# One decoder layer on one core: keys as the standing operand of a small network's first layer, and the last transposes of x1 moved into the last product

## The chip, the cores and the metric

The kernel runs on one core of a Trainium2 chip. The metric is the device time of one execution in microseconds (us); less is better. Each time named is a median of runs, and a trace of one profiled execution is shown beside it. The engines are called PE (TensorE; PEld is its weight load), DVE (VectorE), ACT (ScalarE), POOL (GpSimd) and SP (the queue that starts most DMAs). They run side by side, each works its own list of instructions strictly in order, and they wait for one another by semaphores.

## The reference

One transformer layer over 256 rows of 1024 numbers. What matters here is the compressed branch of mixer A: overlapping blocks of 32 keys (and values) go through a small two-layer network, whose output takes part in an attention. The rest is large products in float32 accuracy.

```python
def compress_blocks(k, pe, w1, w2):
    b, seq, g, d = k.shape
    n_cmp = (seq - CMP_BLOCK) // CMP_STRIDE + 1          # 15 blocks of 32 rows
    idx = jnp.arange(n_cmp)[:, None] * CMP_STRIDE + jnp.arange(CMP_BLOCK)[None, :]
    kb = k[:, idx] + pe[None, None, :, None, :]
    kb = jnp.transpose(kb, (0, 3, 1, 2, 4)).reshape(b, g, n_cmp, CMP_BLOCK * d)
    return jax.nn.gelu(kb @ w1) @ w2                     # (30 rows x 2048) @ (2048 x 64) @ (64 x 64)
...
        kc = compress_blocks(k_c, cmp_pe_k[layer], cmp_k_w1[layer], cmp_k_w2[layer])
        vc = compress_blocks(v_c, cmp_pe_v[layer], cmp_v_w1[layer], cmp_v_w2[layer])
...
        mixed = g_nsa * (y_nsa @ w_up_nsa[layer]) + g_moba * (y_moba @ w_up_moba[layer])
        x = x + mixed @ w_out[layer]
        h2 = rmsnorm(x, norm2_g[layer])
        u = jax.nn.relu(h2 @ w_ff1[layer])
        x = x + (u * u) @ w_ff2[layer]
    return rmsnorm(x, norm_f_g)
```

## The kernel before

**Chunks and slots.** All weights come in 60 chunks of up to 1 MB (`CHUNKS`), one after another: kva, kvb, q, qm, km, vm, gm, upn, upm, wout, ff1, ff2. A chunk is loaded into `raw` (three buffers), then split into a high part `whi` by ACT (line 107) and a low part `wlo` by DVE (line 109), so that three fast products give float32 accuracy (`mm3`, line 214). One *slot* is the run of matmuls that uses one chunk (24 or 48 of them), and it also carries the splitting of the chunk two further on. "Slot 5" is the slot of chunk 5.

**The order is written by hand.** `at(pos, f)` puts work at a share `pos` of the slot, and `run_slot` emits it between the slot's matmuls, in order of `pos`. Each engine's list is therefore what these shares make it: what stands ahead in an engine's list is done first, even while it waits.

**The small network.** `cmp_gather` (slot 3) transposes the keys and values of kva and adds the position term; the result is `kE`, 30 blocks by 16 pairs of rows, for keys (s=0) and values (s=1). `cmp_mlp1` (share 0.7 of slot 4) multiplies by `w1`: 32 float32 products with 64 columns of `w1` standing in the array and 30 columns of `kE` moving, keys in the first 64 columns of the array and values in the other 64, one sum each. Behind it come an ACT copy to `gl`, three DVE operations, a tanh on ACT and one DVE operation that writes `glr`: the gelu. `cmp_mlp2` (0.45 of slot 5) takes `glr` through the second layer: one product for the keys (`tk`, read by DVE into `bdk`) and one for the values (`tv`, read into `bdv`). A float32 product is recorded as two matmuls, a transpose as one.

**Around it in slots 4 and 5.** `split(5, ..)` and `split(6, ..)` on DVE; `transp_k(kva)` (0.1 of slot 5) transposes the keys `ks` on PE, and `split_evac` reads them out on ACT (`ksh`, `ks`) and DVE (`ksl`); `rope` on DVE; `transp_k(kvb)` (0.75 of slot 5) does the same for `kw`.

**Banks.** Small results share two PSUM banks, `tp` and `yb`, which `tp_tile` gives out in turn; large ones take the banks in `turn["acc"]`, in turn as well. A bank's next user waits until its last one has been read. `tv` is two calls behind the `ks` transposes and so falls on their bank. For the gm slots (from chunk 12) the bank `tp` joins `acc0` and `acc1`, behind them.

**x1.** `x1_rows` transposes the new residual back to rows, four 128x128 transposes for each quarter: quarter 0 in the middle of the second wout slot, quarters 1 to 3 in the middle of the second ff2 slot.

Of the kernel before, what the change touches and what calls it, by code (L numbers as in the profile page):

```python
# [33 lines left out]


K_MASK, K_COS, K_SIN, K_CMP, K_BDK, K_BDV, K_IND, K_N = 0, 128, 160, 192, 222, 254, 382, 386
S_PE, S_W2, S_N = 0, 32, 160


@with_exitstack  # L40
def hybrid_layer(ctx: ExitStack, tc: tile.TileContext, gxd, w, w1c, small, const, gf, out):
# [82 lines left out]
    sm = cp.tile([128, S_N], F32, name="sm")  # L124
    kc_ = cp.tile([128, K_N], F32, name="kc")

    glr = ap_.tile([128, 4, 32], F32, name="glr")
    pcs = ap_.tile([128, 2, 4, 32], F32, name="pcs")
    pool.memset(glr, 0.0)
    pool.memset(pcs, 0.0)  # L130
    w1 = ap_.tile([128, 2, 16, 64], F32, name="w1", tag="w1")
    xsq = ap_.tile([128, 8, 256], F32, name="xsq", tag="early")
# [12 lines left out]
    load(4)  # L145
    g1, g2 = gx[:, 0:8], gx[:, 8:16]
    pe_sb = sm[:, S_PE:S_PE + 32].rearrange("p (s l) -> p s l", s=2)
    w2 = sm[:, S_W2:S_W2 + 128]
    cmask = kc_[:, K_MASK:K_MASK + 128]
    cos = kc_[:, K_COS:K_COS + 32].rearrange("p (t d) -> p t d", t=2)  # L150
    sin = kc_[:, K_SIN:K_SIN + 32].rearrange("p (t d) -> p t d", t=2)
# [107 lines left out]
            split_events(c, (0.0, 0.45), (0.3, 0.46))  # L259


    kva = ap_.tile([128, 2, 128], F32, name="kva")
    kcd = ap_.tile([128, 2, 4, 2, 64], F32, name="kcd")
    kvb = ap_.tile([128, 2, 408], F32, name="kvb")
    vm = ap_.tile([128, 2, 512], F32, name="vm")
# [58 lines left out]
        split_evac(tp[:, None, 0:256], dst, False)  # L324


    kE = ap_.tile([128, 2, 16, 30], F32, name="kE")
    bdk = ap_.tile([128, 32], F32, name="bdk")
    bdv = ap_.tile([128, 4, 128], F32, name="bdv")
    sT = ap_.tile([128, 256], F32, name="sT")  # L330
    pcT = ap_.tile([128, 256], F32, name="pcT")
    gl = ap_.tile([128, 3, 30], F32, name="gl")
    gates = (ap_.tile([128, 56], F32, name="gates")[:, 0:48]
             .rearrange("p (b q t h) -> p b q t h", b=3, q=4, t=2))
    U = {}
# [1 line left out]
    def cmp_gather(s):  # L337
        tp = tp_tile()
        for g in range(2):
            for t in range(2):  # L340
                pe.transpose(tp[:, g * 256 + t * 128:g * 256 + t * 128 + 128],
                             kcd[:, t, 2 * s + g].rearrange("p a d -> p (a d)"), ident)
        for l2 in range(2):
            p0 = l2 * 64
            v = tp[p0:p0 + 64].rearrange("p (g i l m) -> p g l i m", g=2, l=8, m=2)
            for lh in range(2):
                ls = slice(lh * 8, (lh + 1) * 8)
                o = kE[p0:p0 + 64, s, ls, :].rearrange("p l (g i) -> p g l i", g=2)
                dve.tensor_tensor(
                    o, v[:, :, :, lh:lh + 15, l2],  # L350
                    pe_sb[p0:p0 + 64, s, None, ls, None].to_broadcast([64, 2, 8, 15]),
                    op=ALU.add)

    def cmp_mlp1():
        tp = tp_tile()
        for l in range(16):
            for s in range(2):
                mm(tp[s * 64:(s + 1) * 64, 0:30], w1[:, s, l, :], kE[:, s, l, :], l == 0, l == 15)
        act.activation(gl[:, 0], tp[:, 0:30], AF.Copy)
        dve.tensor_tensor(gl[:, 1], gl[:, 0], gl[:, 0], op=ALU.mult)  # L360
        dve.tensor_scalar(gl[:, 1], gl[:, 1], 0.044715, 1.0, op0=ALU.mult, op1=ALU.add)
        dve.tensor_tensor(gl[:, 1], gl[:, 1], gl[:, 0], op=ALU.mult)
        act.activation(gl[:, 2], gl[:, 1], AF.Tanh, scale=0.7978845608028654)
        a, b = (gl[:, i, None, :].to_broadcast([128, 4, 30]) for i in (2, 0))
        dve.scalar_tensor_tensor(glr[:, :, 0:30], a, 1.0, b, op0=ALU.add, op1=ALU.mult)

    def cmp_mlp2():
        tk = tp_tile()
        mm(tk[:, 0:32], w2[0:64, :], glr[0:64, 0, :], True, True)
        dve.tensor_tensor(bdk, tk[:, 0:32], kc_[:, K_BDK:K_BDK + 32], op=ALU.mult)  # L370
        tv = tp_tile()
        mm(tv[:, 0:128], glr[64:128].rearrange("k p c -> k (p c)"), w2[64:128, :], True, True)
        for p in range(4):
            dve.scalar_tensor_tensor(bdv[:, p, :], tv[:, 0:128], kc_[:, K_IND + p:K_IND + p + 1],
                                     kc_[:, K_BDV:K_BDV + 128], op0=ALU.mult, op1=ALU.mult)
# [8 lines left out]
    qT = ap_.tile([128, 4, 256], F32, name="qT")  # L384
    qrT, qmT, kmT = (qk_tiles(n, 4, n != "km") for n in ("qr", "qm", "km"))
    ksT, kwT = (qk_tiles(n, 1, False) for n in ("ks", "kw"))
    st4 = ap_.tile([128, 136], F32, name="st4")[:, 0:64].rearrange("p (a b) -> p a b", a=4)

    def cmp_scores():
        tp = tp_tile()  # L390
        for p in range(4):
            mm(tp[32 * p:32 * p + 32, 0:256], bdk, qT[:, p, :], True, True)
        act.activation(sT, tp[:, 0:256], AF.Copy)

    def cmp_softmax():
        tp = tp_tile()
        for t in range(2):
            pe.transpose(tp[:, t * 128:(t + 1) * 128], sT[:, t * 128:(t + 1) * 128], ident)
        s4 = tp[:, 0:256].rearrange("q (t p c) -> q t p c", t=2, p=4)[:, :, :, 0:30]
        heads = lambda a: a.rearrange("q p (h i) -> q p h i", h=2)  # L400
        for t in range(2):
            dve.tensor_tensor(heads(pcs[:, t, :, 0:30]), heads(s4[:, t]),
                              cmpm[:, t, None, None, :].to_broadcast([128, 4, 2, NCMP]), op=ALU.add)
        s = pcs.rearrange("q t p c -> q (t p) c")[:, :, 0:30].rearrange("q a (h i) -> q a h i", h=2)
        col = lambda i: st4[:, i].rearrange("q (a h) -> q a h", h=2)
        row = lambda i: col(i)[:, :, :, None].to_broadcast([128, 8, 2, NCMP])
        dve.tensor_reduce(col(0), s, op=ALU.max, axis=AX)
        dve.tensor_scalar(st4[:, 0], st4[:, 0], -1.0e30, None, op0=ALU.max)
        dve.tensor_tensor(s, s, row(0), op=ALU.subtract)
        act.activation(s, s, AF.Exp, scale=0.125)  # L410
        dve.tensor_reduce(col(1), s, op=ALU.add, axis=AX)
        dve.tensor_scalar(st4[:, 1], st4[:, 1], 1.0e-30, None, op0=ALU.max)
        dve.reciprocal(st4[:, 2], st4[:, 1])
        dve.tensor_tensor(st4[:, 3].rearrange("q (t p h) -> q t p h", t=2, p=4),
                          st4[:, 2].rearrange("q (t p h) -> q t p h", t=2, p=4),
                          gates[:, 0].rearrange("q p t h -> q t p h"), op=ALU.mult)
        dve.tensor_tensor(s, s, row(3), op=ALU.mult)
# [127 lines left out]
    for sec, c0, n in groups:  # L545
# [6 lines left out]
        for i in range(2):  # L552
            c = c0 + i
            if c == 0:
                at(0.6, load, 5)
            elif c == 1:
                at(0.88, row_squares, 0)
                at(0.88, row_sums, 0, 2, 2)
                for k in range(4):
                    at(0.89, split, 2, k, 4)  # L560
                at(1.1, row_squares, 1)
                at(1.1, row_sums, 4, 6, 2)
                at(1.1, row_sums, 0, 4, 2)
                at(1.1, row_sums, 0, 1, 1)
                for k in range(4):
                    at(1.2, split, 3, k, 4)
                at(1.3, load, 6)
                at(1.3, nc.sync.dma_start, w1, w1c)
            elif c == 2:
                at(0.75, row_norm)  # L570
            elif c == 3:
                for t in range(2):
                    at(0.0, evac_tm, "kva", t, first[t], 384)
                for k in range(2):
                    at(0.1, split, 4, k, 2, "h")
                at(0.45, cmp_gather, 0)
                for k in range(2):
                    at(0.5, split, 4, k, 2, "l")
                at(0.51, load, 7)
                at(0.6, cmp_gather, 1)  # L580
                for k in range(2):
                    at(0.7, split, 5, k, 2, "h")
            elif c == 4:
                for t in range(2):
                    at(0.0, evac_tm, "kvb", t, second[t], 408)
                at(0.1, split, 5, 0, 2, "l")
                at(0.2, rope, kva, 2)
                at(0.3, split, 5, 1, 2, "l")
                at(0.35, load, 8)
                split_events(c, (0.5, 0.55), (0.8, 0.9))  # L590
                at(0.7, cmp_mlp1)
            else:
                std_events(c)
            unit_events(c)
# [42 lines left out]
                       scale=hrstd[:, t:t + 1])  # L637

    prev = []
    turn["acc"].append("tp")  # L640
    for g in range(4):
        accs = [acc_tile(), acc_tile()]
        for i in range(2):
# [133 lines left out]
    for i in range(4):  # L777
# [11 lines left out]
            at(0.02, f, *a)  # L789
        if i == 1:  # L790
            at(0.01, open_ff)

            at(26 / 48 - 0.001, lambda: x1_rows([0], [bank("yb", "yb")]))
            at(0.9, lambda: act.dma_start(FB["gfb"], gf[None, :].to_broadcast([128, 1024])))
        if i == 3:
            outs = [acc_tile()[:, 0:256] for _ in range(2)]
# [101 lines left out]
    for i in range(15):  # L898
# [2 lines left out]
            at(0.02, f, *a)  # L901
        prev = []
        if i == 1:
            at(0.5, x1_rows, range(1, 4), [acc_tile() for _ in range(3)])
        if i == 3:
            at(0.1, rstd2)
        if i < 14:
# [23 lines left out]
def _layout(np, inp):  # L931
# [26 lines left out]
    xT = np.asarray(inp["x"])[0].T.reshape(8, 128, 256).transpose(1, 0, 2).reshape(128, 2048)  # L958
    gx = np.concatenate(cols + [xT], 1)
    cols = [np.asarray(inp[n])[0].reshape(16, 128).T for n in ("cmp_pe_k", "cmp_pe_v")]  # L960
    w2 = np.concatenate([np.asarray(inp[n])[0] for n in ("cmp_k_w2", "cmp_v_w2")], 0)
    cols += [w2, w2]
    small = np.concatenate(cols, 1)

    t = np.arange(256)
# [39 lines left out]
```

## Time and profile before

| | |
|---|---|
| median of 3 runs | 386.05 us (385.52 to 386.81) |
| the profiled execution's own time | 386.25 us |
| its span, first to last instruction | 384.4 us |
| PE busy | 375.2 us, 98% of the span |
| PEld busy | 329.1 us, 86% |
| DVE busy | 254.3 us, 66% |
| ACT busy | 205.6 us, 54% |
| POOL busy | 3.2 us, 1% |
| DMA | 66.31 MB |

The span leaves 1.85 us of the profiled time outside. Busy shares are averages over stages with different limits. A matmul's end is modelled, so matmuls that follow each other closely overlap in the rows; what a matmul costs in a stream is the distance of its start from the next start.

### The profile page before, as it was taken

Reading aid. Unit: us, or ns where it says so; the run is one execution under the profiler, and the core shown is the slowest. Engines: PE = TensorE matmul, PEld = TensorE weight load, DVE = VectorE, ACT = ScalarE, POOL = GpSimd, SP = SyncE. Lnnn points to the kernel's source line nnn. Section 1 sums busy time; section 2 is a strip of 40 time slices with the busy share of each in tenths; the row PEclk is TensorE's granted clock in tenths of the full one; section 3 lists DMA queues with packets and bytes.
Section 4 is the critical chain, followed back from the end, with each engine's and each line's share of the span. In section 5 each row is a group of like instructions: output and inputs, shape, how many; then the busy total and the mean of one; then the engine's idle time right before and its main releaser. Section 6 shows DMA issues by size and latency. Waiting matters only on the chain.

```text
span 384.4 us, 5939 instructions
## 1 busy us (share of the span) xinstructions
PE 375.2 (98%) x2404; PEld 329.1 (86%) x2404; DVE 254.3 (66%) x396; ACT 205.6 (54%) x359; POOL 3.2 (1%) x14
## 2 busy tenths in 40 slices
PE   7999999999999999999999999999999999999993
PEld 6897778878888788779999999999998888888883
DVE  3969788887966869567857656756757354344435
ACT  5974465766746747353554555565565364323412
POOL 1000000000000000000000000000000000000000
PEclk9999999999999999999999999999999999999999
DMA  7977535333533434630756644554564546545003
GB/s 243 368 304 231 208 124 205 109 111 124 206 109 112 124 140 175 217 112 7 264 224 219 220 160 175 215 188 155 206 213 143 206 186 237 198 162 188 0 2 110
DMA packets 11261, 66.31 MB, mean 173 GB/s; under 512 B 1249, under 2 KB 2785, under 8 KB 3937
## 3 DMA queue, kind: packets, MB, share of 16 engines
q1 hardware_dynamic: 10800, 65.14, 47.5%
q10 hardware_dynamic: 432, 0.79, 0.6%
q8 instruction: 19, 0.31, 0.3%
q14 instruction: 10, 0.07, 0.1%
HBM read 64.87 MB, written 1.05 MB: 172 GB/s over the span
## 4 chain that ended last, share of the span: by engine, by line
PE 90%; DVE 3%; ACT 2%; issue 2%; DMA 1%; SPq 1%; POOLq 0%; POOL 0%; DVEq 0%; ACTq 0%
PE acc L212 54%; PE o L212 21%; PE qacc L212 3%; PE yb L212 3%; PE kvbacc L212 2%; DMA raw<-in_kva_dram 1%; DVE wlo L109 1%; PE Sa L212 1%; PE Sa L493 1%; PE Sb L493 1%; ACT whi L107 1%; PE tp L293 1%; PE Sb L212 1%; PE tp L212 1%; DVE hTl L168 0%
## 5 line engine op out<-in xcount | busy, mean ns | idle before, releaser
L107 ACT ACTIVATE whi<-raw 128x1024 fp32r<-128x1024 f32 (+2 forms) x128 | 123.2, 991 | 99.6 <-PE o L212 35.5
L109 DVE TENSOR_TENSOR wlo<-raw,whi 128x1024 fp32r<-128x1024 f32 (+2 forms) x128 | 141.6, 1137 | 43.8 <-ACT whi L107 43.6
L212 PE MATMUL acc<-h2h,whi 128*128 128x256 f32 x256 | 71.9, 281 | 0.0
L212 PE MATMUL acc<-h2l,whi 128*128 128x256 f32 x256 | 71.9, 281 | 0.0
L212 PE MATMUL acc<-h2h,wlo 128*128 128x256 f32 x256 | 71.9, 281 | 0.0
L212 PE MATMUL acc<-whi,hTh 128*128 128x512 f32 (+1 forms) x128 | 51.2, 400 | 0.9 <-ACT whi L107 0.5
L212 PE MATMUL acc<-wlo,hTh 128*128 128x512 f32 (+1 forms) x128 | 51.1, 399 | 0.4 <-DVE wlo L109 0.2
L212 PE MATMUL acc<-whi,hTl 128*128 128x512 f32 (+1 forms) x128 | 49.8, 389 | 0.0
L212 PE MATMUL o<-whi,sqh 128*128 128x512 f32 (+1 forms) x128 | 49.5, 386 | 0.0
L212 PE MATMUL o<-whi,sql 128*128 128x512 f32 (+1 forms) x128 | 49.4, 386 | 0.0
L212 PE MATMUL o<-wlo,sqh 128*128 128x512 f32 (+1 forms) x128 | 49.4, 386 | 0.0
L212 PEld LDWEIGHTS acc<-h2h,wlo 128*128 128x128 f32 x256 | 49.2, 192 | 0.0
L212 PEld LDWEIGHTS acc<-h2h,whi 128*128 128x128 f32 x256 | 48.1, 188 | 0.0
L212 PEld LDWEIGHTS acc<-h2l,whi 128*128 128x128 f32 x256 | 48.1, 188 | 0.0
L212 PEld LDWEIGHTS acc<-whi,hTh 128*128 128x128 f32 x128 | 24.3, 190 | 7.9 <-ACT whi L107 1.3
L212 PEld LDWEIGHTS acc<-wlo,hTh 128*128 128x128 f32 x128 | 24.3, 190 | 5.4 <-DVE wlo L109 1.5
L212 PEld LDWEIGHTS o<-whi,sql 128*128 128x128 f32 x128 | 24.0, 188 | 4.9
L212 PEld LDWEIGHTS o<-wlo,sqh 128*128 128x128 f32 x128 | 24.1, 188 | 4.8
L212 PEld LDWEIGHTS o<-whi,sqh 128*128 128x128 f32 x128 | 24.0, 188 | 4.7
L212 PEld LDWEIGHTS acc<-whi,hTl 128*128 128x128 f32 x128 | 24.4, 190 | 4.2
L816 DVE TENSOR_TENSOR ur<-ur 128x512 f32<-128x512 f32 x16 | 11.1, 693 | 20.6 <-ACT ur L815 19.4
L818 DVE TENSOR_TENSOR sql<-ur,sqh 128x512 fp32r<-128x512 f32 x16 | 11.1, 692 | 11.2 <-ACT sqh L817 11.2
(245 smaller groups left out, 513.5 us busy)
## 6 DMA issues: line engine op xcount, KB each, us to landing
raw<-in_ff_dram SPq DMA_DIRECT2D x32, 1024.0 KB, 4.8
raw<-in_gm_dram SPq DMA_DIRECT2D x8, 1024.0 KB, 4.8
raw<-in_wout_dram SPq DMA_DIRECT2D x4, 1024.0 KB, 4.8
raw<-in_q_dram SPq DMA_DIRECT2D x2, 1024.0 KB, 5.9
raw<-in_qm_dram SPq DMA_DIRECT2D x2, 1024.0 KB, 5.3
raw<-in_km_dram SPq DMA_DIRECT2D x2, 1024.0 KB, 4.9
raw<-in_vm_dram SPq DMA_DIRECT2D x2, 1024.0 KB, 4.8
raw<-in_upn_dram SPq DMA_DIRECT2D x2, 1024.0 KB, 4.8
```

The lines of the kernel that those rows point to most:

```text
L107: act.activation(hi[c][:, a:b], raw[c][:, a:b], AF.Copy)
L109: dve.tensor_tensor(lo[c][:, a:b], raw[c][:, a:b], hi[c][:, a:b].bitcast(F32), op=ALU.subtract)
L212: pe.matmul(o, l, r, start=start, stop=stop, skip_group_check=True)
L293: pe.transpose(tp[:, j * 256 + t * 128:j * 256 + t * 128 + 128], src[:, t, (2 * i + j) * 128:(2 * i + j + 1) * 128], ident)
L493: pe.transpose(S[x][:, j, c:c + 128], P[:, 2 * x + j, c:c + 128], ident)
L816: dve.tensor_tensor(rf, rf, rf, op=ALU.mult)
L818: dve.tensor_tensor(l, rf, h.bitcast(F32), op=ALU.subtract)
```

## The change

Three edits, one launch as before.

1. The first layer of the small network: `kE`, padded to 32 columns and cleared by POOL once, now stands in the array, and 64 columns of `w1` move. The 32 products go in turn to four groups of 32 columns of the array: two for keys, two for values, even and odd pairs of rows. ACT copies the 128 rows to `hid`, and a new function, `cmp_gelu` (0.92 of slot 4), adds even and odd and transposes by two small products with the identity; the gelu then works on 64 rows of 64 columns, with two last operations for `glr` in place of one. `w2` lies on 64 rows for both halves (64 KB more to load with `small`).
2. Quarter 0 of `x1_rows` moves to the others in the second ff2 slot.
3. In the gm slots the bank `tp` comes ahead of `acc0` and `acc1`. `sT` takes the space of `kva`, for room.

```diff
-    glr = ap_.tile([128, 4, 32], F32, name="glr")
+    glr = ap_.tile([64, 2, 4, 32], F32, name="glr")
+    kE = ap_.tile([128, 2, 16, 32], F32, name="kE")
...
+    pool.memset(kE, 0.0)
...
     def cmp_mlp1():
+
         tp = tp_tile()
         for l in range(16):
             for s in range(2):
-                mm(tp[s * 64:(s + 1) * 64, 0:30], w1[:, s, l, :], kE[:, s, l, :], l == 0, l == 15)
-        act.activation(gl[:, 0], tp[:, 0:30], AF.Copy)
+                g = 32 * (2 * (l % 2) + s)
+                mm(tp[g:g + 32, 0:64], kE[:, s, l, :], w1[:, s, l, :], l < 2, l >= 14)
+        act.activation(hid, tp[:, 0:64], AF.Copy)
+
+    def cmp_gelu():
+
+        tp = tp_tile()
+        for i in range(2):
+            mm(tp[0:64, 0:64], hid, ident[:, 64 * i:64 * i + 64], i == 0, i == 1)
+        act.activation(gl[:, 0], tp[0:64, 0:64], AF.Copy)
         dve.tensor_tensor(gl[:, 1], gl[:, 0], gl[:, 0], op=ALU.mult)
         dve.tensor_scalar(gl[:, 1], gl[:, 1], 0.044715, 1.0, op0=ALU.mult, op1=ALU.add)
         dve.tensor_tensor(gl[:, 1], gl[:, 1], gl[:, 0], op=ALU.mult)
         act.activation(gl[:, 2], gl[:, 1], AF.Tanh, scale=0.7978845608028654)
-        a, b = (gl[:, i, None, :].to_broadcast([128, 4, 30]) for i in (2, 0))
-        dve.scalar_tensor_tensor(glr[:, :, 0:30], a, 1.0, b, op0=ALU.add, op1=ALU.mult)
+        for s in range(2):
+            a, b = (gl[:, i, None, 32 * s:32 * s + 30].to_broadcast([64, 4, 30]) for i in (2, 0))
+            dve.scalar_tensor_tensor(glr[:, s, :, 0:30], a, 1.0, b, op0=ALU.add, op1=ALU.mult)
 
     def cmp_mlp2():
         tk = tp_tile()
-        mm(tk[:, 0:32], w2[0:64, :], glr[0:64, 0, :], True, True)
+        mm(tk[:, 0:32], w2[:, 0, :], glr[:, 0, 0, :], True, True)
...
-        mm(tv[:, 0:128], glr[64:128].rearrange("k p c -> k (p c)"), w2[64:128, :], True, True)
+        mm(tv[:, 0:128], glr[:, 1].rearrange("k p c -> k (p c)"), w2[:, 1, :], True, True)
...
                 split_events(c, (0.5, 0.55), (0.8, 0.9))
                 at(0.7, cmp_mlp1)
+                at(0.92, cmp_gelu)
...
-    turn["acc"].append("tp")
+    turn["acc"].insert(0, "tp")
...
-            at(26 / 48 - 0.001, lambda: x1_rows([0], [bank("yb", "yb")]))
...
-            at(0.5, x1_rows, range(1, 4), [acc_tile() for _ in range(3)])
+            at(0.5, x1_rows, range(4), [acc_tile() for _ in range(3)] + [bank("yb", "yb")])
```

Because `cmp_gelu` stands at 0.92 of slot 4, behind the low parts of chunk 6 (0.8 and 0.9), DVE's list changes at the end of slot 4. Before (the first `wlo` is chunk 5's, the two behind `glr` are chunk 6's):

```order
L109 TENSOR_TENSOR wlo<-raw,whi 128x1024 [waits Activation_49]
L360 TENSOR_TENSOR gl<-gl 128x30 [waits Activation_49]
L361 TENSOR_SCALAR gl<-gl 128x30 [waits DVE_49]
L362 TENSOR_TENSOR gl<-gl 128x30 [waits DVE_49]
L365 SCALAR_TENSOR_TENSOR glr<-gl 128x4x30 [waits Activation_49,Pool_49]
L109 TENSOR_TENSOR wlo<-raw,whi 128x1024 [waits DMAHW0_49,PE_49]
L109 TENSOR_TENSOR wlo<-raw,whi 128x1024
L382 TENSOR_SCALAR gates<-gates 128x48 [waits Activation_49]
L312 TENSOR_TENSOR ksl<-tp,ksh 128x256 [waits PE_49,Activation_49]
```

And in the change:

```order
L109 TENSOR_TENSOR wlo<-raw,whi 128x1024 [waits Activation_49]
L109 TENSOR_TENSOR wlo<-raw,whi 128x1024 [waits DMAHW0_49,PE_49,Activation_49]
L109 TENSOR_TENSOR wlo<-raw,whi 128x1024 [waits Activation_49]
L370 TENSOR_TENSOR gl<-gl 64x64 [waits Activation_49]
L371 TENSOR_SCALAR gl<-gl 64x64 [waits DVE_49]
L372 TENSOR_TENSOR gl<-gl 64x64 [waits DVE_49]
L376 SCALAR_TENSOR_TENSOR glr<-gl 64x4x30 [waits Activation_49]
L376 SCALAR_TENSOR_TENSOR glr<-gl 64x4x30
L393 TENSOR_SCALAR gates<-gates 128x48 [waits Activation_49]
L314 TENSOR_TENSOR ksl<-tp,ksh 128x256 [waits PE_49,Activation_49]
```

The two low parts of chunk 6 now stand ahead of the gelu; `gates` and `ksl` follow as before.

ACT's list at the same place, in the change (the first `gl` is the copy out of PSUM, the second the tanh; `whi` is the first half of chunk 7):

```order
L362 ACTIVATE hid<-tp 128x64 [waits PE_49]
L369 ACTIVATE gl<-tp 64x64 [waits PE_49]
L373 ACTIVATE gl<-gl 64x64 [waits DVE_49]
L107 ACTIVATE whi<-raw 128x1024 [waits DMAHW2_49,PE_49,Activation_49]
L391 ACTIVATE gates<-kvb 128x12x2 [waits Activation_49] x2
L312 ACTIVATE ksh<-tp 128x256 [waits PE_49]
L313 ACTIVATE ks_191<-tp 128x128
```

Nothing moved there but the new `hid`: the tanh stands ahead of `whi`, `gates` and the `ks` copies, as before.

On PE, with buffer numbers, the first matmuls of the gm slots (`acc_961` is the first result). Before:

```order
L212 MATMUL acc_797<-whi_706,hTl_130 128x512
L212 MATMUL acc_961<-whi_798,hTh_129 128x512 [waits Activation_49]
L212 MATMUL acc_961<-wlo_799,hTh_129 128x512
L212 MATMUL acc_961<-whi_798,hTl_130 128x512
L212 MATMUL acc_961<-whi_798,hTh_129 128x512
```

And in the change:

```order
L214 MATMUL acc_804<-whi_713,hTl_132 128x512
L214 MATMUL acc_968<-whi_805,hTh_131 128x512 [waits DVE_49]
L214 MATMUL acc_968<-wlo_806,hTh_131 128x512
L214 MATMUL acc_968<-whi_805,hTl_132 128x512
L214 MATMUL acc_968<-whi_805,hTh_131 128x512
```

The first result's bank was the one that ACT reads `vm` out of, and is now the one that DVE reads `kml` out of.

## Rows read from the trace of the kernel before

**Rows 1.** The page's chain that ended last, share of the span by engine.

```profile
PE 90%; DVE 3%; ACT 2%; issue 2%; DMA 1%; SPq 1%; POOLq 0%; POOL 0%; DVEq 0%; ACTq 0%
```

**Rows 2.** Timeline of PE, first layer: start us, us, engine, line, what, count.

```profile
30.93 2.06 PE L212 MATMUL tp<-kE,w 128*64 128x30 f32 x64
32.91 0.50 PE L212 MATMUL qacc<-whi,hTl 128*128 128x512 f32 x1
```

**Rows 3.** Timeline of PE in slot 5, around `cmp_mlp2`.

```profile
36.93 0.39 PE L212 MATMUL qacc<-whi,hTh 128*128 128x512 f32 x1
37.15 0.39 PE L212 MATMUL qacc<-wlo,hTh 128*128 128x512 f32 x1
...
37.89 0.50 PE L212 MATMUL qacc<-whi,hTl 128*128 128x512 f32 x1
```

**Rows 4.** Timeline of DVE, 31.9 to 40 us.

```profile
31.96 1.22 DVE L109 TENSOR_TENSOR wlo<-raw,whi 128x1024 fp32r<-128x1024 f32 x1
33.26 0.19 DVE L360 TENSOR_TENSOR gl<-gl 128x30 f32<-128x30 f32 x1
...
34.46 2.35 DVE L109 TENSOR_TENSOR wlo<-raw,whi 128x1024 fp32r<-128x1024 f32 x2
...
36.95 0.42 DVE L312 TENSOR_TENSOR ksl<-tp,ksh 128x256 fp32r<-128x256 f32 x1
...
39.54 0.18 DVE L370 TENSOR_TENSOR bdk<-tp,kc 128x32 f32<-128x32 f32 x1
```

**Rows 5.** Timeline of PEld in slot 5, at the transposes of `kw`.

```profile
39.77 0.20 PEld L323 LDWEIGHTS tp<-ident,kvb 128*128 128x128 f32 x2 [0.43 <-DVE bdk L370]
```

**Rows 6.** Timeline at the first matmul of the gm slots.

```profile
85.40 0.68 DVE L312 TENSOR_TENSOR kml<-tp,kmh 128x512 fp32r<-128x512 f32 x1
...
85.57 0.72 ACT L273 ACTIVATE vm<-acc,rstd 128x512 f32<-128x512 f32 x1
...
86.34 0.50 PE L212 MATMUL acc<-whi,hTh 128*128 128x512 f32 x1 [0.40 <-ACT vm L273]
```

**Rows 7.** Groups of float32 matmuls with 64 standing columns: busy us, mean ns | idle.

```profile
L212 PE MATMUL yb<-PT,kvb 128*64 128x256 f32 x32 | 5.0, 392 | 0.0
L212 PE MATMUL yb<-PT,kvb 128*64 128x128 f32 x32 | 3.1, 273 | 0.0
```

**Rows 8.** Timeline of PE, window 48.58 to 48.62, `cmp_scores` with 32 standing columns.

```profile
48.59 0.42 PE L212 MATMUL tp<-qT,bdk 128*32 128x256 f32 x4
```

**Rows 9.** Timeline of ACT, 33 to 37 us, idle before in brackets.

```profile
33.92 0.23 ACT L363 ACTIVATE gl<-gl 128x30 f32<-128x30 f32 x1 [0.70 <-DVE gl L362]
34.89 1.06 ACT L107 ACTIVATE whi<-raw 128x1024 fp32r<-128x1024 f32 x1 [0.74 <-PE qacc L212]
...
36.34 0.27 ACT L311 ACTIVATE ks<-tp 128x128 f32<-128x128 f32 x1
```

**Rows 10.** The chain that ended last, transposes of x1: start us, us.

```profile
184.93 0.44 PE yb L773 x4
...
297.88 1.31 PE acc L773 x12
```

**Rows 11.** The tile `kE`, who writes it: ns min/median/max, first and last start.

```profile
L349 DVE TENSOR_TENSOR kE<-tp,sm x8: 390/402/411, 24.3 to 29.3; 64x240 f32<-64x240 f32 x8
```

**Rows 12.** DMA issues, the load of `small`: KB, median us from issue to landing.

```profile
sm<-in_small_dram SPq DMA_DIRECT2D x1, 80.0 KB, 7.7
```

**Rows 13.** Timeline of PE at the start, products of one shape.

```profile
6.13 0.52 PE L212 MATMUL acc<-wlo,hTh 128*128 128x384 f32 x1
6.45 0.52 PE L212 MATMUL acc<-whi,hTl 128*128 128x384 f32 x1
...
9.22 0.44 PE L212 MATMUL acc<-whi,hTh 128*128 128x384 f32 x1 [0.45 <-ACT whi L107]
...
10.27 0.35 PE L212 MATMUL acc<-whi,hTh 128*128 128x384 f32 x1
10.46 0.34 PE L212 MATMUL acc<-wlo,hTh 128*128 128x384 f32 x1
```

More of the change, by code (lines that the diff above doesn't have):

```diff
@@ L36 @@
 K_MASK, K_COS, K_SIN, K_CMP, K_BDK, K_BDV, K_IND, K_N = 0, 128, 160, 192, 222, 254, 382, 386
-S_PE, S_W2, S_N = 0, 32, 160
+S_PE, S_W2, S_N = 0, 32, 288
 @with_exitstack
@@ L147, in hybrid_layer @@
     pe_sb = sm[:, S_PE:S_PE + 32].rearrange("p (s l) -> p s l", s=2)
-    w2 = sm[:, S_W2:S_W2 + 128]
+    w2 = sm[0:64, S_W2:S_W2 + 256].rearrange("p (s c) -> p s c", s=2)
     cmask = kc_[:, K_MASK:K_MASK + 128]
@@ L259, in std_events @@
             split_events(c, (0.0, 0.45), (0.3, 0.46))
-    kva = ap_.tile([128, 2, 128], F32, name="kva")
+    kva = ap_.tile([128, 2, 128], F32, name="kva", tag="kva")
     kcd = ap_.tile([128, 2, 4, 2, 64], F32, name="kcd")
@@ L324, in transp_k @@
         split_evac(tp[:, None, 0:256], dst, False)
-    kE = ap_.tile([128, 2, 16, 30], F32, name="kE")
+    hid = ap_.tile([128, 64], F32, name="hid")
     bdk = ap_.tile([128, 32], F32, name="bdk")
     bdv = ap_.tile([128, 4, 128], F32, name="bdv")
-    sT = ap_.tile([128, 256], F32, name="sT")
     pcT = ap_.tile([128, 256], F32, name="pcT")
-    gl = ap_.tile([128, 3, 30], F32, name="gl")
+    gl = ap_.tile([64, 3, 64], F32, name="gl")
     gates = (ap_.tile([128, 56], F32, name="gates")[:, 0:48]
@@ L347, in cmp_gather @@
                 ls = slice(lh * 8, (lh + 1) * 8)
-                o = kE[p0:p0 + 64, s, ls, :].rearrange("p l (g i) -> p g l i", g=2)
+                o = kE[p0:p0 + 64, s, ls, 0:30].rearrange("p l (g i) -> p g l i", g=2)
                 dve.tensor_tensor(
@@ L386, in hybrid_layer @@
     ksT, kwT = (qk_tiles(n, 1, False) for n in ("ks", "kw"))
-    st4 = ap_.tile([128, 136], F32, name="st4")[:, 0:64].rearrange("p (a b) -> p a b", a=4)
+    st4 = ap_.tile([128, 104], F32, name="st4")[:, 0:64].rearrange("p (a b) -> p a b", a=4)
     def cmp_scores():
@@ L392, in cmp_scores @@
             mm(tp[32 * p:32 * p + 32, 0:256], bdk, qT[:, p, :], True, True)
-        act.activation(sT, tp[:, 0:256], AF.Copy)
+        U["sT"] = ap_.tile([128, 256], F32, name="sT", tag="kva")
+        act.activation(U["sT"], tp[:, 0:256], AF.Copy)
     def cmp_softmax():
@@ L397, in cmp_softmax @@
         for t in range(2):
-            pe.transpose(tp[:, t * 128:(t + 1) * 128], sT[:, t * 128:(t + 1) * 128], ident)
+            pe.transpose(tp[:, t * 128:(t + 1) * 128], U["sT"][:, t * 128:(t + 1) * 128], ident)
         s4 = tp[:, 0:256].rearrange("q (t p c) -> q t p c", t=2, p=4)[:, :, :, 0:30]
@@ L960, in _layout @@
     cols = [np.asarray(inp[n])[0].reshape(16, 128).T for n in ("cmp_pe_k", "cmp_pe_v")]
-    w2 = np.concatenate([np.asarray(inp[n])[0] for n in ("cmp_k_w2", "cmp_v_w2")], 0)
-    cols += [w2, w2]
+    w2 = [np.asarray(inp[n])[0] for n in ("cmp_k_w2", "cmp_v_w2")]
+    w2 = np.concatenate([w2[0], w2[0], w2[1], w2[1]], 1)
+    cols += [np.concatenate([w2, np.zeros_like(w2)], 0)]
     small = np.concatenate(cols, 1)
```

## The prediction

> **What bounds the kernel now.** I read the page first. The chain that ended last lies on PE for nine tenths of the span [rows 1]: from the first weights to the last product PE goes from one matmul to the next. So an edit pays what it takes off PE's list or out of PE's few waits, and it costs whatever makes PE wait, since a microsecond lost there is not made up by anyone. Then I read the timelines of the three places that the change touches, and at each asked who the engine behind PE would be.
>
> The first layer holds PE from 30.93 to 32.91 us [rows 2], 1.98 us for 64 records. Its two groups of columns run beside each other, so each has 32 records in that time, 62 ns each. A little later PE, DVE and ACT are nearly level: PE comes to the second layer at 37.38 (the start at 37.15 plus 0.23, about the distance of the 512-column products before it) and goes on at 37.89 [rows 3], while the `ksl` that `tv` needs ends at 36.95 + 0.42 = 37.37 [rows 4]. There is no slack at all in this place. At 39.77 the transposes of `kw` are let go by `bdk` on DVE, 0.23 after its start at 39.54 [rows 4, 5]. At 86.34 PE has waited 0.40 us for ACT to read `vm` out of the bank [rows 6].
>
> **The first layer: -0.97 us of PE.** A float32 record takes 392 ns with 256 moving columns and 273 with 128 [rows 7], so a moving column costs 119/128 = 0.93 ns, and 64 of them 60 ns. The weight load of 32 columns cannot take longer than that of 64 did, which was no more than 62 ns with everything. In the change each of four groups has 16 records: 16 x 60 = 0.96 us plus the 0.06 that the old one had over 32 x 60, together 1.01 against 1.98. That needs the groups to run beside each other. The rows show it for this form: four records of 32 standing columns, each about 390 ns long, start and end within 0.42 us [rows 8], so within 0.03 us of each other. Bounds: nothing, if 64 records keep the 31 ns that they have on average now, and 1.05 if the rest of 0.06 goes too.
>
> A rule speaks against it. The Trainium skill, "TensorE: Matmul & The Clock Gate", section "Wait — 56ns, not 53.3ns?", says that start to start never drops below about 25 ns, however narrow the matmul. By it 64 records take an estimated 1.6 us and the term is -0.38. The row of four starts in 0.03 us, over three distances of 10 ns at most, does not agree, and I go by the row.
>
> **The sum of even and odd: +0.40 us of PE.** Two float32 products, four records in one group of columns, so one after the other: 4 x 60 = 0.24 us. The four records of the second layer, put between two large products, push the next one from 37.38 to 37.89, by 0.51 [rows 3]. I take 0.40 between these bounds.
>
> So PE would come to the second layer at 37.38 - 0.97 + 0.40 = 36.81.
>
> **The gelu behind two low parts: this is where the gain goes.** Before, the gelu runs on DVE at 33.26, as soon as `gl` is there, and the low parts of chunk 6 follow at 34.46 for 2.35 us [rows 4]. In the change they stand ahead (DVE's list above). Their high parts are done and the buffer is free by then, so they start right behind the low part of 31.96. The pitch of such an operation is 2.35 - 1.22 = 1.13, so 33.09 and 34.22, and the next operation starts at 35.4, a little before the second ends.
>
> - DVE: three operations on `gl` from 35.4. From the first to the tanh it was 33.92 - 33.26 = 0.66 [rows 4, 9]; with 64 columns for 30 I take 0.70. The tanh starts at 36.10.
> - ACT: it has been standing at the tanh since it copied `gl` (about 34), and behind the tanh wait `whi` of chunk 7, `gates` and the two `ks` copies (ACT's list above). `whi` follows at about 36.3. From its start to the end of `ks` it was 36.34 + 0.27 - 34.89 = 1.72 [rows 9]: 38.02.
> - DVE: `ksl` waits for the `ks` copy and starts at 38.05 in place of 36.95, 1.10 later. Between `ksl` and `bdk` DVE is busy without a gap, with the same operations (2.59 us, [rows 4]), so `bdk` is 1.10 later too.
> - PE: `tv` cannot start before `ksl` has read its bank, at about 38.05 + 0.42 + 0.05 = 38.5. PE is there at 36.8 and has `tk` to do; it stands for about 1.5 us. Behind it waits all of PE. The transposes of `kw` then wait for `bdk`: 39.77 + 1.10.
>
> So from there on PE is **1.10 us later than before**, and the two terms above don't enter: PE comes to this place before 38.5 whether the first layer takes 1.0 or 2.0 us. Bounds: +0.8, if the gelu's chain keeps its 0.66, PE goes on 0.3 behind the release of `tv` and `bdk` is hidden; +1.4, if each of the small operations is 0.06 longer and the second `glr` operation (0.28 us) falls between. From then on DVE and PE are late by the same amount and ACT waits for PE again, so I see nothing that widens or gives it back.
>
> **The bank of the first gm result: -0.21 us.** PE now waits for `kml`, which ends at 85.40 + 0.68 = 86.08, and not for `vm`, which ends at 85.57 + 0.72 = 86.29 [rows 6]. Bounds: 0 and -0.40, the whole wait. The bank of `vm` is needed half a slot later.
>
> **x1: 0.** Four transposes leave the wout slot, where they take 0.44 us, and join twelve that take 1.31, 0.109 each [rows 10]. The fourth copy lies on ACT, busy 54%, and the sums of squares that read x1 come more than a slot later. If the cover were gone, it would cost one copy, some 0.6 us of ACT.
>
> **POOL and DMA: 0.** `kE` is first written at 24.3 us [rows 11], and POOL has 3.2 us of work in the whole span, so a clearing that is four times as wide as that of `pcs` ends long before. `small` takes 7.7 us to land with 80 KB [rows 12]; even 1.8 times as long is early for 24.3.
>
> **Sum.** 1.10 - 0.21 = +0.89. The profiled execution's 386.25 becomes 387.14. It lies 0.20 above the median of the runs shown, so on that median I forecast 386.05 + 0.89 = **386.9 us**, 0.23% more. A measurement of this kernel can tell about 0.3% (1.16 us) from no change, so this is "the same", close to the edge.
>
> **Rivals.**
>
> *The gain reaches the end.* If `tv` did not wait for `ksl` (the two low parts run before PE gets there, or ACT is not held by the tanh), the terms on PE count: -0.97 + 0.40 - 0.21 = -0.78, 385.3 us. For it: no row of before shows such a wait. Against it: the two lists above, and durations that all have rows. With every bound in its favour (-1.05 + 0.24 - 0.40 = -1.21, 384.8) it is only just faster by 0.3%. So it gives little to "faster". By the 25 ns of the Trainium skill, "TensorE: Matmul & The Clock Gate" (the section named above), this rival would end at -0.38 + 0.40 - 0.21 = -0.19, 385.9 us, an estimate.
>
> *Slower: PE's clock falls in the new wait.* At the start PE runs on the lower level of its clock (1.2 of 2.4 GHz): 384 columns in 0.32 us, later in 0.19 [rows 13]. There it stood for 0.45 us before 9.22 and was on the higher level afterwards [rows 13]. No row shows what a wait of 1.5 us does; if the clock fell behind it, each microsecond at the lower level would lose 0.4, and some 3 us of it 1.2: 388.1 us. It decides where a stand of 1.5 us is too long.
>
> *The groups don't run beside each other.* Then the first layer stays at up to 1.98 us, PE comes to `tv` at 37.8, still before 38.5, and the time is the same 386.9.
>
> **How the numbers follow.** The wait for `ksl` as worked out: 0.76, between 386.3 and 387.6 with its bounds and what runs scatter; about a third of it lies above the 387.2 from which it counts as slower. The gain reaches the end: 0.12, mostly within 0.3%. The clock falls: 0.12, slower. Scatter of single runs and what no case holds add a little at both ends. So faster 0.05, the same 0.60, slower 0.35. The range reaches from the middle of the first rival to just short of the other: 385.5 to 388.0.
>
> **What would show it.** In the profile after: the first layer in about 1.0 us, with four records starting together; the two `wlo` ahead of `gl` on DVE, and `gl` at 35.4; ACT idle until about 36.1 before the tanh; on PE a wait of about 1.5 us before the second product of `cmp_mlp2`, put down to `ksl`; `bdk` 1.1 us later than now; the wait at the first gm matmul some 0.2 us shorter and put down to `kml`. It is wrong if PE's wait in slot 5 is under 0.5 us, if PE makes up time later, or if matmuls behind the wait run at 0.32 us for 384 columns' worth.

## The result and the profile after

The changed kernel takes **383.09 us** (median of 22 runs) against 386.06 for the kernel before: a ratio of 0.9942, 95% interval 0.9918 to 0.9967, so 0.6% faster. I had forecast 386.9 and 0.05 for faster. The executions of the kernel after fall into two groups: 16 took 382.3 to 384.1 us (median 382.86), six 386.5 to 388.3. The ratios here and below follow the means rather than the medians, and leave out executions more than 1.5% above the fastest of their kernel: the one of 388.3 us here, and two of the run e11 below. The traced execution took 384.06 us, with a span of 382.3.

The small network first, since the prediction spoke mostly of it. Timeline of PE in the kernel after (start us, us, engine, line, what): the first layer, the sum of even and odd, and slot 5.

```profile
32.02 1.10 PE L214 MATMUL tp<-w,kE 128*32 128x64 f32 x64
33.05 0.50 PE L214 MATMUL qacc<-whi,hTl 128*128 128x512 f32 x1
...
34.32 0.39 PE L214 MATMUL qacc<-wlo,hTh 128*128 128x512 f32 x1
34.64 0.45 PE L214 MATMUL tp<-ident,hid 128*64 128x64 f32 x4
35.01 0.50 PE L214 MATMUL qacc<-whi,hTl 128*128 128x512 f32 x1
...
38.20 0.41 PE L214 MATMUL tp<-glr,sm 64*128 64x32 f32 x2
39.53 0.49 PE L214 MATMUL tp<-sm,glr 64*128 64x128 f32 x2 [0.93 <-DVE ksl L314]
39.95 0.50 PE L214 MATMUL qacc<-whi,hTl 128*128 128x512 f32 x1
```

The same stretch on DVE and ACT, and on PEld at the transposes of `kw`:

```profile
33.04 3.49 DVE L109 TENSOR_TENSOR wlo<-raw,whi 128x1024 fp32r<-128x1024 f32 x3
36.45 0.21 DVE L370 TENSOR_TENSOR gl<-gl 64x64 f32<-64x64 f32 x1
...
39.05 0.42 DVE L314 TENSOR_TENSOR ksl<-tp,ksh 128x256 fp32r<-128x256 f32 x1 [0.24 <-ACT ks L313]
...
37.16 0.26 ACT L373 ACTIVATE gl<-gl 64x64 f32<-64x64 f32 x1 [1.83 <-DVE gl L372]
...
41.89 0.20 PEld L325 LDWEIGHTS tp<-ident,kvb 128*128 128x128 f32 x2 [0.48 <-DVE bdk L381]
```

Everything in this trace is 1.09 us later when the first layer begins (32.02, was 30.93 [rows 2]). That belongs to this execution, as the clock below shows: in the run after_again the first layer begins at 31.13. Counted from the first layer's start, the first layer needs 1.03 us in place of 1.98. The gelu on DVE stands behind three `wlo`, `ksl` runs at 39.05, and PE waits for it. The next large product is 39.95 - 37.89 - 1.09 = 0.97 us later than before [rows 3], the transposes of `kw` 41.89 - 39.77 - 1.09 = 1.03 us [rows 5]. That is the loss that I forecast, 1.10, within 0.13 us.

At the first gm matmul PE now waits 0.20 us, and for `kml` (before 0.40, for `vm` [rows 6]):

```profile
87.49 0.68 DVE L314 TENSOR_TENSOR kml<-tp,kmh 128x512 fp32r<-128x512 f32 x1
...
88.23 0.50 PE L214 MATMUL acc<-whi,hTh 128*128 128x512 f32 x1 [0.20 <-DVE kml L314]
```

Up to here the kernel after is 88.23 - 86.34 = 1.89 us behind. At the end it is 2.1 ahead (span 382.3 against 384.4). So I followed the chain that ended last through wout, ff1 and ff2. Before (start us, us, engine, tile, line, count):

```profile
179.08 5.85 PE acc L212 x49
...
185.36 104.35 PE acc L212 x886
289.72 8.16 PE o L212 x36
...
299.19 73.48 PE o L212 x324
372.67 0.03 issue
```

And after:

```profile
180.94 106.25 PE acc L214 x935
287.19 8.18 PE o L214 x36
295.37 1.31 PE acc L786 x12
296.68 0.44 PE yb L786 x4
297.12 73.48 PE o L214 x324
370.60 0.02 issue
```

The same 935 products of 256 columns (49 + 886) took 289.72 - 179.08 = 110.64 us with the four transposes among them, and take 106.25 without. Take 0.44 for the transposes themselves off, and 3.95 us are left, with not one product fewer. Behind the transposes a product cost 104.35 / 886 = **117.8 ns**, start to start. The whole stretch of the kernel after has 106.25 / 935 = 113.6. The products of 512 columns in ff2 did not change: 73.48 us for 324 in both. No wait stands in either row; the products themselves follow each other at another distance. The group of these products shows it too, the page of before and of after:

```profile
L212 PE MATMUL acc<-h2h,whi 128*128 128x256 f32 x256 | 71.9, 281 | 0.0
```

```profile
L214 PE MATMUL acc<-h2h,whi 128*128 128x256 f32 x256 | 70.7, 276 | 0.0
```

The clock is not it. The granted clock is the share of its full speed that PE was given in a stretch. The stretches of the kernel after (busy us and instructions of each engine, then the granted clock, DMA share, GB/s) show 1.00 behind the new wait and in ff1; only the start of this execution is lower, 0.94:

```profile
0.00:31.00 31.00, 28.36 (x137) 26.66 (x138) 19.45 (x40) 22.38 (x40) 3.09 (x13) 0.94 0.82 290
31.00:45.00 14.00, 13.02 (x119) 9.65 (x118) 11.80 (x35) 5.86 (x15) 0.00 (x0) 1.00 0.57 219
45.00:86.00 41.00, 41.00 (x245) 32.74 (x244) 33.56 (x74) 23.55 (x50) 0.00 (x0) 1.00 0.43 154
190.00:220.00 30.00, 30.00 (x267) 30.00 (x266) 21.12 (x30) 17.07 (x25) 0.00 (x0) 1.00 0.64 229
```

The kernel before has 1.00 in the same stretch of ff1, with 257 products in place of 267:

```profile
190.00:220.00 30.00, 30.00 (x257) 30.00 (x256) 19.77 (x27) 16.19 (x23) 0.00 (x0) 1.00 0.62 228
```

The late start has its cause in the first 14 us, where the granted clock is 0.88 in this execution and 1.00 in the traces of before and after_again. PE, and then the stretch from 10 to 14 us:

```profile
9.39 0.44 PE L214 MATMUL acc<-whi,hTh 128*128 128x384 f32 x1 [1.15 <-ACT whi L107]
...
10.88 0.52 PE L214 MATMUL acc<-wlo,hTh 128*128 128x384 f32 x1
11.20 0.52 PE L214 MATMUL acc<-whi,hTl 128*128 128x384 f32 x1
```

```profile
10.00:14.00 4.00, 4.00 (x14) 4.00 (x15) 4.00 (x10) 4.00 (x10) 0.00 (x0) 0.57 1.05 423
```

PE had stood for 1.15 us ahead of 9.39, and soon behind it the products of 384 columns start 0.32 us apart, the distance of the lower level [rows 13]. In after_again PE stood for 1.00 us at this place and the clock stayed. So this execution lost about a microsecond at its start.

### The profile page after: what moved, and what is told of

The parts are those of the page before. It is cut to its first block, busy times and chain, and to the rows that moved or that the text cites. A ratio compares the mean times of both kernels' runs of the same rounds, so it can differ in the third digit from the quotient of the medians.

```text
span 382.3 us, 5945 instructions
## 1 busy us (share of the span) xinstructions
PE 371.9 (97%) x2408; PEld 326.4 (85%) x2408; DVE 254.5 (67%) x397; ACT 205.6 (54%) x360; POOL 4.2 (1%) x15
## 3 DMA queue, kind: packets, MB, share of 16 engines
HBM read 64.94 MB, written 1.05 MB: 173 GB/s over the span
## 4 chain that ended last, share of the span: by engine, by line
PE 85%; DVE 7%; ACT 2%; issue 2%; DMA 2%; SPq 1%; POOLq 0%; POOL 0%; DVEq 0%; ACTq 0%
PE acc L214 54%; PE o L214 21%; DVE wlo L109 3%; PE yb L214 2%; PE kvbacc L214 2%; DMA raw<-in_kva_dram 2%; ACT whi L107 1%; PE Sa L505 1%; PE Sb L505 1%; PE Sa L214 1%; PE Sb L214 1%; DVE kE L350 1%; PE tp L295 1%; PE qacc L214 0%; PE acc L786 0%
## 5 line engine op out<-in xcount | busy, mean ns | idle before, releaser
L214 PE MATMUL acc<-h2h,whi 128*128 128x256 f32 x256 | 70.7, 276 | 0.0
L214 PE MATMUL acc<-h2l,whi 128*128 128x256 f32 x256 | 70.7, 276 | 0.0
L214 PE MATMUL acc<-h2h,wlo 128*128 128x256 f32 x256 | 70.7, 276 | 0.0
L214 PE MATMUL acc<-whi,hTl 128*128 128x512 f32 (+1 forms) x128 | 50.6, 395 | 0.0
L214 PEld LDWEIGHTS acc<-h2h,wlo 128*128 128x128 f32 x256 | 48.0, 188 | 0.0
```

The lines of the kernel that those rows point to most:

```text
L214: pe.matmul(o, l, r, start=start, stop=stop, skip_group_check=True)
```

## The experiments

The theory: x1's four transposes throw the 256-column products behind them from 113.4 to 117.8 ns, and the products keep that until their shape changes; the second edit takes the transposes out and gains 4 us, while the rest of the change costs what I had forecast. The expectations below call this the pitch theory; pitch is the distance from start to start. The rivals: the gain is the turn of the banks, or the small network with its new layout.

**One part of the change at a time.** e1 is the kernel before with the second edit alone, e2 with the first alone (and `sT` in the space of `kva`, which makes room for it), e3 with the new turn of the banks alone; e4 is the kernel after with the second edit undone, so with the first and third.

```diff
 # e1, against before
-            at(26 / 48 - 0.001, lambda: x1_rows([0], [bank("yb", "yb")]))
...
-            at(0.5, x1_rows, range(1, 4), [acc_tile() for _ in range(3)])
+            at(0.5, x1_rows, range(4), [acc_tile() for _ in range(3)] + [bank("yb", "yb")])
```

> The kernel before with the second edit alone: the four transposes of x1's quarter 0 leave the wout slot. Pitch theory (the transposes throw the 256-column products behind them from a distance of 113.3 ns to 117.8 ns, start to start, until the shape of the products changes; some 880 products by 4.5 ns are 4.0 us): 382.1 us, and a distance of 113.3 in wout and ff1. Rival, the bank in the gm slots or the small network gives the gain: 386.05, and 117.8.

> The change with the first edit alone (the small network, with its room and layout); x1's quarter 0 stays in the wout slot and the gm bank as before. Pitch theory: 386.05 + 1.0 = 387.0 us, 117.8 ns in ff1. Rival, the small network gives the gain: 382 to 383, 113.3 ns.

> The kernel before with the third edit alone (the bank tp ahead of acc0 and acc1 in the gm slots). Pitch theory: 386.05 - 0.2 = 385.85 us, 117.8 ns in ff1. Rival, the turn of the banks gives the gain: 382 us, 113.3 ns.

> The kernel after with the second edit undone: quarter 0 of x1 is transposed in the wout slot again. Pitch theory: 386.05 + 1.0 - 0.2 = 386.9 us, 117.8 ns from behind the transposes on. Rivals, the small network or the bank gives the gain: 383 us, as the kernel after, 113.3 ns.

| | us, median | ratio to before, 95% |
|---|---|---|
| e1: second edit | 381.96 | 0.9895, 0.9881 to 0.9908 |
| e2: first edit | 386.82 | 1.0025, 1.0016 to 1.0034 |
| e3: third edit | 385.65 | 0.9992, 0.9981 to 1.0002 |
| e4: first and third | 386.61 | 1.0018, 1.0009 to 1.0027 |

Before was 385.97 beside them. The second edit alone gives -4.01 us; the first costs 0.85; the third gives 0.32, within its interval of nothing. e4 is my forecast of 386.9 within 0.3 us. The chain of e4 shows both distances beside each other: 4.09 / 36 = 113.6 ns ahead of the transposes and 104.35 / 886 = 117.8 behind.

```profile
180.97 4.09 PE acc L214 x36
185.06 0.44 PE yb L786 x4
185.49 104.35 PE acc L214 x886
```

Both rivals have fallen.

**Does it hang on the place?** e6 puts the transposes of before one product earlier or later. e9 is e1 with four transposes of the identity, read by nobody, at x1's old place; e7 is the kernel after with the same in the fifth ff1 slot; e10 is the kernel before with x1's own transposes moved to that ff1 slot.

```diff
 # e9, against e1 (e7: the same stir() at that share of ff1 slot i == 4)
+    def stir():
+        t = bank("yb", "yb")
+        for k in range(4):
+            pe.transpose(t[:, k * 128:(k + 1) * 128], ident, ident)
...
+            at(26 / 48 - 0.001, stir)
 # e10, in the ff1 loop
+        if i == 4:
+            at(26 / 48 - 0.001, lambda: x1_rows([0], [bank("yb", "yb")]))
```

> The kernel before with x1's quarter 0 one product earlier in the wout slot. If any four transposes between these products leave the longer distance behind them: 386.05 us, 117.8 ns. If it hangs on which product they come in front of: 382.1 us, 113.3 ns.

> The kernel before with x1's quarter 0 one product later in the wout slot. If any four transposes between these products leave the longer distance behind them: 386.05 us, 117.8 ns. If it hangs on which product they come in front of: 382.1 us, 113.3 ns.

> The kernel after with four transposes of the identity, whose result nobody reads, in the middle of the fifth ff1 slot. If such transposes throw the stream into the longer distance: 0.44 us for themselves and 4.5 ns for each of the some 550 products of ff1 behind them, 2.5 us: 382.9 + 2.9 = 385.8 us, 113.3 ns ahead of them and 117.8 behind. If only x1's place in wout does it: 383.3 us, 113.3 ns throughout.

> The kernel before with the second edit, and four transposes of the identity, whose result nobody reads, at the place in the wout slot where x1's quarter 0 stood. If the place makes the pitch: 382.0 + 0.44 + 4.0 = 386.4 us, 117.8 ns behind them. If it is what x1's transposes read or wait for: 382.4 us, 113.3 ns.

> The kernel before with x1's quarter 0 in the middle of the fifth ff1 slot. If it is what x1's transposes read: 382.0 + 2.5 = 384.5 us, 113.3 ns ahead of them and 117.8 behind. If the place makes the pitch: 382.0 us, 113.3 ns throughout.

Measured: e6 385.78 and 386.03 us (before 386.00), and 104.47 / 887 and 104.23 / 885 = 117.8 ns behind the transposes, so it does not hang on which of these three products follows. e7 382.88 us, with 62.35 / 550 = 113.4 ns behind the transposes of the identity. e9 382.47, e10 384.62. The chains of e9 and e10:

```profile
185.30 0.44 PE yb L780 x4
185.74 100.43 PE acc L212 x886
```

```profile
180.99 42.05 PE acc L212 x371
223.04 0.44 PE yb L773 x4
223.48 64.78 PE acc L212 x550
```

Behind the identity at x1's own place the 886 products run at 100.43 / 886 = 113.4 ns. Behind x1's transposes in ff1 550 products run at 64.78 / 550 = 117.8, and the 371 ahead of them at 113.3. So neither the place nor a pause of four transposes makes the longer distance. Something about x1's transposes does; that any four transposes would do it, one of the two cases of e6 and e7, has fallen with e7 and e9.

**Can it be brought back?** e8 is the kernel before with the identity's transposes in ff1, behind x1's in wout.

> The kernel before with four transposes of the identity, whose result nobody reads, in the middle of the fifth ff1 slot. If a second disturbance brings the stream back to 113.3 ns: 386.0 + 0.44 - 2.5 = 383.9 us. If the stream keeps what the wout slot left: 386.4 us, 117.8 ns on both sides of them.

384.22 us (before 386.16; nine of its ten executions 383.9 to 384.7): the products behind the second disturbance get the shorter distance back, by the time. No trace shows it, since the traced execution is the tenth, of 387.96 us, at a granted clock of 0.95 from 14 us on. It has the longer distance on both sides of the identity's transposes, and already ahead of x1's, 5.30 / 45 = 117.8 ns:

```profile
181.00 5.30 PE acc L212 x45
186.30 0.44 PE yb L773 x4
186.74 39.58 PE acc L212 x336
```

Its products of 512 columns keep 8.16 / 36 = 226.7 ns. So the longer distance can also come without x1's transposes ahead of it; here it came with the lower granted clock, which the other traces with 117.8 ns do not have in ff1.

**What about x1's transposes?** Their standing operand lies in `gx`, which starts 32 bytes past a multiple of 64 in the program's layout; the identity and `sga` (transposed in the first wout slot; the products behind it run at 113.4 ns in before) start at a multiple. That follows from the sizes of the tiles; no trace shows an address. e11 is the kernel before with 8 columns of padding ahead of `gx`, and 8 fewer in the gap behind it. e12 transposes a copy of the identity (one ACT operation more) 32 bytes off at x1's old place, e14 the same copy 8 columns further.

```diff
 # e11, against before
-    kc_ = cp.tile([128, K_N], F32, name="kc")
+    kc_ = cp.tile([128, K_N + 8], F32, name="kc")[:, 0:K_N]
...
-    cp.tile([128, 104], F32, name="gap0")
+    cp.tile([128, 96], F32, name="gap0")
 # e12, against e9 (e14: [:, 8:136])
+    def copy_id():
+        FB["id2"] = FB["p"].tile([128, 144], F32, name="id2")[:, 0:128]
+        act.activation(FB["id2"], ident, AF.Copy)
...
-            pe.transpose(t[:, k * 128:(k + 1) * 128], ident, ident)
+            pe.transpose(t[:, k * 128:(k + 1) * 128], FB["id2"], ident)
```

> The kernel before, x1's quarter 0 in the wout slot as there; only the tile gx, in which x1 lies, starts 32 bytes higher (8 columns of padding in front of it, 8 fewer in the gap behind it, nothing else moves), so that x1's rows start at a multiple of 64 bytes, as the identity's and sga's do. If the standing operand's place in memory makes the pitch: 382.0 us, 113.3 ns behind the transposes. If it is anything else about x1's transposes (their waits, their data): 386.05 us, 117.8 ns.

> As e9 (x1 all in ff2, four transposes of an identity at the old place in the wout slot), but of a copy of the identity that starts 32 bytes past a multiple of 64. If the standing operand's place makes the pitch: 382.5 + 4.0 = 386.4 us, 117.8 ns behind them. If not: 382.5 us, 113.3 ns.

> As e12, the same copy of the identity in the same tile, but 8 columns further, so that it starts at a multiple of 64 bytes. If the standing operand's place makes the pitch: 382.5 us, 113.3 ns. If it is the copy, or the tile, that makes it: 386.4 us, 117.8 ns.

e11: **382.32 us** against 386.13, ratio 0.9903 (0.9882 to 0.9924), with the transposes still in the wout slot. Its chain has the shorter distance behind them, 100.43 / 886 = 113.4 ns:

```profile
184.71 0.44 PE yb L773 x4
185.15 100.43 PE acc L212 x886
```

That shift of 32 bytes is the only edit, and it is worth nearly as much as taking the transposes out (3.8 us against 4.0). The other engines that read and write `gx` are not the cause: in e1 it lies where it did, only the transposes are gone, and the distance is the shorter one. But it does not hold every time: three of its 12 executions took 385.8 to 387.2 us, the others 381.4 to 383.2. e12 fell in halves: six of 12 at 382.2 to 382.9, six at 386.2 to 387.1 (median 384.54). e14's six all lie between 381.6 and 384.0. So a standing operand 32 bytes off makes the higher times likelier, for the identity in half of the executions, for x1 in all that I saw (no run of the kernel before was under 385.0, nor of e2, e3, e4 and e6, where x1 is transposed between these products as well).

Whether e12's higher half is the longer distance was to be seen from two more traces of it.

> e12 once more, for a trace: its executions fall near 382.4 us or near 386.5 in equal numbers, and the trace of the first was one of 382.2 (113.3 ns). By the pitch theory an execution near 386.5 shows 117.8 ns from right behind the transposes to the end of ff1, and one near 382.4 113.3 ns. If the 386.5 come from elsewhere (the start, the DMAs, the clock), 113.3 ns in both.

> As the look before it, a second trace of e12: 382.4 us with 113.3 ns or 386.5 us with 117.8 ns from behind the transposes, by the pitch theory; 113.3 ns in both, if the time comes from elsewhere.

They took 383.24 and 383.70 us, and show 113.4 ns. No trace of a higher execution of e12 came, so this stays open, and with it the six higher executions of the kernel after: they have no such transposes in wout, and their granted clock, 0.994 to 0.998, is that of the lower ones. The kernel after itself was run once more:

> The kernel after once more, unchanged, beside the others: whether its executions near 387 us come back. By the pitch theory each execution is near 382.9 us (113.3 ns) or near 386.9 (117.8 ns), and none lies between.

382.81 us, six executions from 382.4 to 384.8; none near 387 came back, and one, of 384.78, lies between the two groups, which the theory did not expect. Its mean granted clock is 0.992, like the 0.991 of the two traced executions whose clock fell in the first 14 us (384.06 of the kernel after, 383.70 of e12); a slow start of that kind is the likely reason, but this execution has no trace.

**The forecast wait, and the best version.** e5 is the kernel after with `cmp_gelu` at 0.79 of slot 4 in place of 0.92, ahead of chunk 6's low parts. e13 is e1 with the third edit.

> The kernel after with the sum of even and odd and the gelu at 0.79 of slot 4, ahead of the low parts of chunk 6. The prediction's own term (the gelu behind two low parts costs PE a wait of 0.93 us for ksl, and 1.0 us in all): the wait is gone, 0.9 to 1.5 us less than the kernel after in an execution at a distance of 113.3 ns, 381.4 to 382.0 us. Rival, another engine is the bound in this place and PE waits as long for it: 382.9, as the kernel after.

> The kernel before with the second and third edits, without the small network's: 382.0 - 0.3 = 381.7 us, 113.3 ns, below both kernels, if the first edit only costs. If it gains as well: above the kernel after, 383 us or more.

e5: 382.44 us, above the 381.4 to 382.0 of its expectation. In PE's timeline the wait for `ksl` is 0.20 and not 0.93, and from the first layer's start at 31.29 to the next large product it takes 7.20 us (kernel after 39.95 - 32.02 = 7.93, before 37.89 - 30.93 = 6.96):

```profile
31.29 1.10 PE L214 MATMUL tp<-w,kE 128*32 128x64 f32 x64
...
38.07 0.48 PE L214 MATMUL tp<-sm,glr 64*128 64x128 f32 x2 [0.20 <-DVE ksl L314]
38.49 0.50 PE L214 MATMUL qacc<-whi,hTl 128*128 128x512 f32 x1
```

And DVE:

```profile
37.59 0.42 DVE L314 TENSOR_TENSOR ksl<-tp,ksh 128x256 fp32r<-128x256 f32 x1
```

So 0.73 us of the loss comes from where `cmp_gelu` stands, less than the 0.9 to 1.5 expected: now DVE, with one operation more, is at `ksl` only at 37.59, and PE still stands. So the first edit is no gain in this form either: 7.20 us against 6.96 before. e13, without it, has 381.85 us, ratio 0.9888 (0.9873 to 0.9904): the fastest of all, 4.3 us below before, though not to be told from e1.

## Why the prediction was wrong

The step that failed is **"x1: 0"**. I costed the four transposes by their own length, 0.44 us that moves from one slot to another, and asked who waits for the copy behind them. Both are right: ff2 is 0.46 us longer (370.60 - 287.19 against 372.67 - 289.72), and nobody waits. What I left out, without asking, is what they do to the 886 products behind them: 4.4 ns each, 3.9 us together. The trace of before would have told it. I read only the transposes' own pieces of the chain [rows 10]; this is what stands right ahead of them there, in the part from 181 us on:

```profile
180.96 3.97 PE acc L212 x35
```

3.97 / 35 is 113.4 ns, and the piece right behind them has 117.8. e1, which takes the transposes out and nothing else, measures this term at -4.01 us. None of my three rivals held it, so the range ended at 385.5. Why the products behind take the longer distance stays open; e11 shows that in most executions it hangs on the place of x1 in memory.

The other steps, one by one:

- *The first layer, -0.97*: 33.05 - 32.02 = 1.03 us, so -0.95. (The prediction's own parts, 0.96 and 0.06, make 1.02 and not 1.01, and the far bound 1.02 in place of 1.05; the term does not enter its sum.) Four groups of 32 columns do run beside each other. 64 records in 1.03 us are 16 ns each, so the rule of about 25 ns between starts (the Trainium skill, "TensorE: Matmul & The Clock Gate", section "Wait — 56ns, not 53.3ns?") does not hold between products in different groups of columns.
- *The sum of even and odd, +0.40*: 35.01 - 34.32 = 0.69 where the distance of 512-column products is 0.23, so 0.46.
- *The gelu behind two low parts*: with the 1.09 us of the late start added to the prediction's times, `gl` was to come at 36.49 (36.45), the tanh at 37.19 (37.16), `ksl` at 39.14 (39.05), `tv` at 39.6 (39.53). PE is 1.03 us later behind it, forecast 1.10. PE's wait was to be about 1.5 us and is 0.93: PE comes to `tk` at 38.20 - 1.09 = 37.11 and not at 36.81, and `tk` holds it for 0.41. The delay does not hang on this, since `ksl` sets it. e2 makes it 0.85 us in the whole.
- *The bank, -0.21*: the wait is 0.20 us shorter. e3 measures -0.32, within its interval of nothing.
- *POOL and DMA, 0*: nothing in the chain names them.
- *The clock falls behind the wait*: it stays at 1.00 behind the 0.93 us. A fall of this kind did come in the traced execution, behind PE's stand of 1.15 us at its start, and cost about a microsecond, where that rival had 1.2: the first layer begins 1.09 us later than in before and 0.89 later than in after_again. *The gain reaches the end* and *the groups don't run beside each other* did not occur.

Together: 0.85 - 0.32 - 4.01 = -3.5 us, by e2, e3 and e1. The kernel after lies 3.0 below before as a median, and 3.2 without its six higher executions.

## What to carry to other kernels

A small operation put into a long stream of equal products is to be costed by the stream behind it as well as by its own length: divide the length of the chain's row by its count, ahead of it and behind it, and compare. Where the two differ, look also at where the inserted operation's operand lies in memory before moving work about; eight columns of padding did here, in nine of twelve executions, what the edit of the order did. And take a change apart: one part of this one costs 0.2%, another gives 1%.

## What was not expected of the hardware

- 256-column products with 128 standing columns follow each other at 113.4 or at 117.8 ns at the same granted clock of 1.00, and keep either for hundreds of products (886 in e9 and in before); those of 512 columns have 73.48 / 324 = 226.8 ns in both kernels. Four transposes between them can change the one into the other. At a granted clock of 0.95 (e8) the longer one came without them.
- Which of the two follows the transposes hangs on 32 bytes in the place of the transposes' standing operand (e11, e12 against e14), mostly but not in every execution. Why a distance persists once it is there, and what decides in the executions that go the other way, no run here shows.
